# Down projection, first three column blocks: the low part of the weights made by ScalarE and an accumulating DMA

## The chip, the cores and the metric

The kernel runs on one core of one Trainium2 chip. The metric is the device time of one execution in microseconds; of several executions the median is taken. The engines are PE (TensorE), DVE (VectorE), ACT (ScalarE), POOL (GpSimd) and SP (SyncE, which here issues every DMA of the kernel before). Each engine runs its own instructions in order and waits for the others by semaphores. The DMA engines, 16 for the core, move data on their own once an issue has reached them.

## The reference

One layer of a streaming encoder on 256 tokens of width 2048, all in float32. Cut to what matters here:

```python
def conv_glu(h, w_up, conv_w, conv_b, w_down):
    ug = h @ w_up                                  # [256, 2 * 5632]
    gate, up = ug[..., :D_FF], ug[..., D_FF:]
    gate = causal_depthwise_conv(gate, conv_w) + conv_b
    return (silu(gate) * up) @ w_down              # [256, 5632] @ [5632, 2048]

def reference(...):
    ...                                            # two token mixers, w_in, projections, w_out
    h = h + conv_glu(rmsnorm(h, norm_ffn), w_up, conv_w, conv_b, w_down)
    return rmsnorm(h, norm_final)
```

The change concerns the last product, with `w_down`.

## The kernel before, in words

Every large product is made of float32 operands that are split in two: hi is the value rounded to the matmul's reduced float32 format (fp32r), lo is the exact rest, value minus hi. `mm3` (lines 87 to 90) then issues three matmuls per pair of tiles: hi times hi, hi times lo, lo times hi. Activations are split once; weights are split as they come.

The weights come in blocks of 1 MiB, [128, 2048] float32, four tiles of 128 rows of the weight matrix (K tiles) by 512 columns each. `load_split` (lines 92 to 103) has SP load one block into a tile `raw` (three buffers), and then for each half of it, [128, 1024], has ACT write hi as a copy of raw (line 80), and DVE write lo as raw minus hi (line 81). The pools of hi and lo have three buffers each, so three halves are in hand at a time, and a half's buffers are used again by the half three later.

`product` (lines 211 to 225) walks over the K tiles of one block of 512 output columns. Each half holds two K tiles; for each, and for each of the two blocks of 128 tokens, `mm3` adds into that token block's PSUM tile: twelve matmuls of 512 columns a half. There the activations' tile (`u` in the trace) is the stationary operand and hi or lo of the weights is the moving one, so of the three matmuls only that of line 89 reads lo.

The down projection is four such column blocks over 44 K tiles, that is 11 weight blocks each. The first three go through `product` (lines 615 to 618), each followed by `residual`, which adds h and squares it. The fourth (lines 627 to 658) is written out by hand, with `load_split` for ten of its blocks and a split of its own for the last. The order of each engine's instructions is set by a scheduler when the program is built, not by the order of the lines alone: the splits for the first halves of the down projection are placed among the last instructions of the up projection, and their matmuls follow its last without a pause.

Of the kernel before, what the change touches and what calls it, by code (L numbers as in the profile page):

```python
# [13 lines left out]
ALU = mybir.AluOpType  # L14
# [16 lines left out]
UNIT = 2048  # L31
WARM = 10  # products of zeros

# columns of the packed per-partition vectors
C_NFFN = 0
# [8 lines left out]
def tile_block(ctx: ExitStack, tc: tile.TileContext, ins, out):  # L44
# [32 lines left out]

# [1 line left out]
    def split(hi, lo, src):  # L79
# [11 lines left out]

    def load_split(src):
        """One 1 MiB block of weights as two halves of (hi, lo), each [P, 1024]."""
        raw = wraw.tile([P, 2048], F32, tag="raw", name=nm("raw"))
        sp.dma_start(raw, src)
        got = []
        for h in range(2):
            r = raw[:, h * 1024 : (h + 1) * 1024]
            hi = wsplit.tile([P, 1024], F32R, tag="hi", name=nm("hi"))
            lo = wsplit.tile([P, 1024], F32R, tag="lo", name=nm("lo"))  # L100
            split(hi, lo, r)
            got.append((hi, lo))
        return got

# [1 line left out]
    def rsqrt(v, n):  # L106
# [11 lines left out]

# [1 line left out]
    side = deque()  # L120
# [8 lines left out]

# [1 line left out]
    warm = const.tile([P, NB], BF16, tag="warm", name="warm")  # L131
# [6 lines left out]

# [1 line left out]
    nmix = const.tile([P, KT], F32, tag="nmix", name="nmix")  # L140
# [31 lines left out]

# [1 line left out]
    trig = const.tile([P, 2 * TB * 64], F32, tag="trig", name="trig")  # L174
# [34 lines left out]

# [1 line left out]
    def product(src, start, nk, lhs_h, lhs_l, ready=None, bank=None):  # L211
        """src[start + i] are blocks of four K tiles; returns one PSUM tile per token block."""
        ps = [(bank or acc_tile)() for _ in range(TB)]
        for g in range(nk // 4):
            halves = [ready[g, 0], ready[g, 1]] if ready else load_split(src[start + g])
            for hf, (wh, wl) in enumerate(halves):
                for j in range(2):
                    kt = g * 4 + hf * 2 + j
                    s = slice(j * NB, (j + 1) * NB)
                    for tb in range(TB):  # L220
                        ah = lhs_h(kt)[:, tb * P : (tb + 1) * P]
                        al = lhs_l(kt)[:, tb * P : (tb + 1) * P]
                        mm3(ps[tb], ah, al, wh[:, s], wl[:, s], kt == 0, kt == nk - 1)
            tick()
        return ps
# [3 lines left out]

# [1 line left out]
    def rotary_block(nb, qk, base, late=False, ready=None, bank=None):  # L231
# [38 lines left out]

# [1 line left out]
    ret_h = [unit(F32R) for _ in range(2)]  # L272
    ret_l = [unit(F32R) for _ in range(2)]

    def retention(half, qk, vh, vl):
        dec = unit()
        sp.dma_start(dec[:, : 4 * 384], ins["decay"][:, half * 4 * 384 : (half + 1) * 4 * 384])
        o_all = unit()
        mv = small.tile([P, 8, 2], F32, tag="mv", name=nm("mv"))
        scores = {}  # L280

        def score(hd):
            q3 = [x[:, hd * T : (hd + 1) * T] for x in qk]
            k3 = [x[:, (4 + hd) * T : (5 + hd) * T] for x in qk]
            ps = aux_tile()
            mm3(ps[:, :T], k3[0][:, :P], k3[1][:, :P], q3[0], q3[1], True, True)
            mm3(ps[:, T : T + P], k3[0][:, P:], k3[1][:, P:], q3[0][:, P:], q3[1][:, P:], True, True)
            s = t2k(384, F32)
            sh = t2k(384, F32R)
            sl = t2k(384, F32R)  # L290
            dve.tensor_tensor(s, ps[:, :384], dec[:, hd * 384 : (hd + 1) * 384], ALU.mult)
            split(sh, sl, s)
            scores[hd] = (sh, sl)

        def output(hd):
            sh, sl = scores.pop(hd)
            po = aux_tile()
            v0 = slice(hd * DV, (hd + 1) * DV)
            v1 = slice(1024 + hd * DV, 1024 + (hd + 1) * DV)
            mm3(po[:, :DV], sh[:, :P], sl[:, :P], vh[:, v0], vl[:, v0], True, True)  # L300
            mm3(po[:, DV:], sh[:, P : 2 * P], sl[:, P : 2 * P], vh[:, v0], vl[:, v0], True, False)
            mm3(po[:, DV:], sh[:, 2 * P :], sl[:, 2 * P :], vh[:, v1], vl[:, v1], False, True)
            for tb in range(TB):
                st = small.tile([P, 6], F32, tag="st", name=nm("st"))
                dve.bn_stats(st, po[:, tb * DV : (tb + 1) * DV])
                dve.bn_aggr(mv[:, hd * 2 + tb, :], st)
            # o_all is [token block][head][channel], as the gate is
            ov = o_all.rearrange("p (b h e) -> p b h e", b=TB, h=4)
            act.activation(ov[:, :, hd, :], po.rearrange("p (b e) -> p b e", b=TB), AF.Copy)

        for hd in range(4):
            side.append(lambda hd=hd: score(hd))
            if hd:
                side.append(lambda hd=hd: output(hd - 1))
        side.append(lambda: output(3))
        return o_all, mv

# [35 lines left out]

    # x and its sums of squares follow the first weights, so the first two blocks leave PSUM late
    for _ in range(KT // 4 + 2):
# [22 lines left out]

# [1 line left out]
    ph, pl = unit(F32R), unit(F32R)  # L380
# [63 lines left out]

# [1 line left out]
    sgp = [unit(), unit()]  # L446
# [6 lines left out]

# [1 line left out]
    mg_h = [unit(F32R) for _ in range(2)]  # L455
# [29 lines left out]

# [1 line left out]
    ht_h = [unit(F32R) for _ in range(2)]  # L487
# [32 lines left out]
    def norm2():  # L520
        ss = small.tile([P, TB], F32, tag="ss", name="ss")
        dve.tensor_reduce(ss, ssq2, mybir.AxisListType.X, ALU.add)
        r2 = rms(ss)
        # 1/rms of each token along the free axis, on all partitions
        pb = aux_tile()
        for tb in range(TB):
            dg = tmp.tile([P, P], F32, tag="dg", name=nm("dg"), bufs=1)
            dve.tensor_scalar(dg, ident, r2[:, tb : tb + 1], None, ALU.mult)
            pe.matmul(pb[:, tb * P : (tb + 1) * P], ones, dg, start=True, stop=True)
        dve.tensor_copy(rb, pb[:, :T])  # L530

    side.append(norm2)

# [1 line left out]
    ah = [unit(F32R) for _ in range((NFF + 7) // 8)]  # L535
    al = [unit(F32R) for _ in range((NFF + 7) // 8)]
    for j in range(NFF):
        # the first pair alternates by halves of K, since the last K tiles of h are still on their way
        ps = [acc_tile() for _ in range(2)] if j == 0 else [acc_tile()] * 2
# [32 lines left out]

# [1 line left out]
    gf = unit()  # L574
# [4 lines left out]
    def residual(tb, nb, ps):  # L579
        """h's block of columns, its squares, and the block times the last gain."""  # L580
        n = NB // 2 if nb == 3 else NB
# [12 lines left out]
    def finish(tb, last):  # L594
# [3 lines left out]
        dve.tensor_scalar(v, ssq3[:, tb, 4:5], 1.0 / D, a, ALU.mult, ALU.add)  # L598
        # the root's reciprocal, and a step of Newton's method on it
        r = small.tile([P, 1], F32, tag="fin_r", name=nm("r"))  # L600
# [14 lines left out]
    for nb in range(3):  # L615
        ps = product(ins["w_down"], nb * 11, NFF, lambda k: kview(ah, k), lambda k: kview(al, k))
        for tb in range(TB):
            residual(tb, nb, ps[tb])
# [5 lines left out]

    # the last block of columns: its last eight K tiles go to one token block, then to the other
    LAST = 8
# [33 lines left out]

# [1 line left out]
def _blocks(w, np):  # L662
    """[K, N] -> [N / 512 * K / 512][partition][four K tiles x 512 columns]."""
    k, n = w.shape
# [8 lines left out]
def _arrays(np, x, norm_mix, w_in, w_pool_group, pool_scale, w_pool_proj, ret_gn_gain,  # L673
# [27 lines left out]
    a["norm_final"] = np.asarray(norm_final).reshape(1, D)  # L701
    # constants
    t = np.arange(T)
# [38 lines left out]
```

## Time and profile before

| | |
|---|---|
| time of the runs, median of 2 (lowest to highest) | 1502.15 us (1502.11 to 1502.2) |
| the profiled execution, span from first to last instruction | 1499.8 us |
| between that span and the median of the runs | 2.35 us |
| DMA in the whole run | 287.17 MB, mean 191 GB/s |
| first matmul of the down projection | at 1251.9 us |
| mean granted TensorE clock | 0.999 |

The profile gives for each engine its busy time, and for groups of instructions their count, mean duration and the idle time before them with what ended it. In rows of the timeline the first number is the start and the second the length, both in microseconds; `<-` in brackets names the instruction whose end released the row. Matmuls overlap, so their spacing, not their length, is what one costs. For the profiled execution the page gives the span; the time around it (start-up before the first instruction and completion after the last) is taken as the 2.35 us of the table.

### The profile page before, as it was taken

How to read it: one execution, taken by the hardware profiler on the slowest of the kernel's cores; microseconds unless marked ns; L12 is line 12 of the kernel's file. 1: busy time of each engine (PE TensorE's matmuls, PEld its weight loads, DVE VectorE, ACT ScalarE, POOL GpSimd, SP SyncE). 2: the span in 40 equal slices, each digit the busy share in tenths (PEclk: the TensorE clock that was granted, in tenths of full speed). 3: DMA queues.
4: the chain of work that ended last, by engine and by line, in shares of the span. 5: the costliest groups of instructions: out<-in, count | busy, mean ns of one | idle time of the engine just before them, and what ended most of it. 6: DMA issues, size and time to landing. Idle time of an engine off the chain costs nothing.

```text
span 1499.8 us, 20866 instructions
## 1 busy us (share of the span) xinstructions
PE 1488.2 (99%) x8694; PEld 1319.2 (88%) x8694; DVE 886.6 (59%) x1142; ACT 676.5 (45%) x811; POOL 0.2 (0%) x4
## 2 busy tenths in 40 slices
PE   9999999999999999999999999999999999999997
PEld 6888888888888888888899999999999998888886
DVE  6765865675444455555666666666666665455454
ACT  6545444464444434435544444444444444344343
POOL 0000000000000000000000000000000000000000
PEclk9999999999999999999999999999999999999999
DMA  9554455464455555655444555445554455555553
GB/s 346 200 213 162 177 202 184 168 226 163 178 189 193 195 196 193 231 194 190 175 181 185 181 186 182 184 182 183 184 182 186 180 186 210 194 196 196 197 193 115
DMA packets 42718, 287.17 MB, mean 191 GB/s; under 512 B 4992, under 2 KB 5632, under 8 KB 9088
## 3 DMA queue, kind: packets, MB, share of 16 engines
q1 hardware_dynamic: 42624, 285.84, 52.1%
q8 instruction: 68, 1.11, 0.3%
q14 instruction: 26, 0.21, 0.0%
HBM read 283.73 MB, written 2.10 MB: 191 GB/s over the span
## 4 chain that ended last, share of the span: by engine, by line
PE 98%; DVE 1%; DMA 0%; ACT 0%; SPq 0%; issue 0%; ACTq 0%
PE acc L88 32%; PE acc L90 31%; PE acc L89 31%; PE aux L89 1%; PE aux L90 1%; PE aux L88 1%; DMA raw<-in_w_in 0%; PE aux L246 0%; PE aux L476 0%; PE aux L339 0%; PE aux L505 0%; DVE lo L81 0%; PE aux L404 0%; ACT hi L80 0%; DVE u L85 0%; PE aux L408 0%
## 5 line engine op out<-in xcount | busy, mean ns | idle before, releaser
L81 DVE TENSOR_TENSOR lo<-raw,hi 128x1024 fp32r<-128x1024 f32 (+1 forms) x526 | 635.2, 1209 | 516.3 <-ACT hi L80 515.6
L80 ACT ACTIVATE hi<-raw 128x1024 fp32r<-128x1024 f32 (+1 forms) x526 | 549.4, 1046 | 694.2 <-PE acc L90 446.6
L88 PE MATMUL acc<-hi,u 128*128 128x512 f32 x1336 | 523.6, 392 | 0.0
L90 PE MATMUL acc<-hi,u 128*128 128x512 f32 x1336 | 520.5, 390 | 0.0
L89 PE MATMUL acc<-lo,u 128*128 128x512 f32 x1336 | 520.2, 389 | 0.0
L88 PE MATMUL acc<-u,hi 128*128 128x256 f32 x1408 | 398.7, 283 | 0.0
L90 PE MATMUL acc<-u,lo 128*128 128x256 f32 x1408 | 398.5, 283 | 0.0
L89 PE MATMUL acc<-u,hi 128*128 128x256 f32 x1408 | 398.4, 283 | 0.0
L90 PEld LDWEIGHTS acc<-hi,u 128*128 128x128 f32 x1336 | 250.8, 188 | 52.9
L89 PEld LDWEIGHTS acc<-lo,u 128*128 128x128 f32 x1336 | 251.0, 188 | 50.9
L88 PEld LDWEIGHTS acc<-hi,u 128*128 128x128 f32 x1336 | 250.9, 188 | 50.2
L89 PEld LDWEIGHTS acc<-u,hi 128*128 128x128 f32 x1408 | 270.3, 192 | 0.0
L88 PEld LDWEIGHTS acc<-u,hi 128*128 128x128 f32 x1408 | 270.3, 192 | 0.0
L90 PEld LDWEIGHTS acc<-u,lo 128*128 128x128 f32 x1408 | 270.3, 192 | 0.0
L556 DVE TENSOR_TENSOR t<-acc,rb 128x512 f32<-128x512 f32 x43 | 29.7, 692 | 26.6 <-PE acc L90 26.6
L80 ACT ACTIVATE u<-t 128x256 fp32r<-128x256 f32 x44 | 18.4, 417 | 52.7 <-DVE t L569 52.7
L81 DVE TENSOR_TENSOR u<-t,u 128x256 fp32r<-128x256 f32 x44 | 18.5, 425 | 19.8 <-ACT u L80 19.4
L84 ACT ACTIVATE u<-aux,vecs 128x256 fp32r<-128x256 f32 x40 | 18.6, 468 | 23.1 <-DVE u L85 22.1
L85 DVE SCALAR_TENSOR_TENSOR u<-aux,vecs,u 128x256 fp32r<-128x256 f32 x40 | 19.1, 480 | 8.7 <-ACT u L84 8.7
L567 DVE SCALAR_TENSOR_TENSOR t<-t,vecs,t 128x254 f32<-128x254 f32 x44 | 21.3, 483 | 1.6
L568 ACT ACTIVATE t<-t,vecs 128x256 f32<-128x256 f32 x44 | 21.9, 497 | 0.0
L566 DVE SCALAR_TENSOR_TENSOR t<-t,vecs,t 128x255 f32<-128x255 f32 x44 | 21.1, 478 | 0.0
(129 smaller groups left out, 457.8 us busy)
## 6 DMA issues: line engine op xcount, KB each, us to landing
raw<-in_w_up SPq DMA_DIRECT2D x88, 1024.0 KB, 4.8
raw<-in_w_in SPq DMA_DIRECT2D x84, 1024.0 KB, 4.8
raw<-in_w_down SPq DMA_DIRECT2D x44, 1024.0 KB, 4.8
raw<-in_w_ret_proj SPq DMA_DIRECT2D x16, 1024.0 KB, 4.8
raw<-in_w_out SPq DMA_DIRECT2D x16, 1024.0 KB, 4.8
raw<-in_w_pool_proj SPq DMA_DIRECT2D x8, 1024.0 KB, 4.8
u<-in_x SPq DMA_DIRECT2D x4, 1024.0 KB, 8.1
raw<-in_w_in SPq DMA_DIRECT2D x7, 512.0 KB, 7.8
```

Source lines behind the costliest of these rows:

```text
L80: act.activation(hi, src, AF.Copy)
L81: dve.tensor_tensor(lo, src, plain(hi), ALU.subtract)
L84: act.activation(hi, src, AF.Copy, scale=scale)
L85: dve.scalar_tensor_tensor(lo, src, scale, plain(hi), ALU.mult, ALU.subtract)
L88: pe.matmul(o, ah, bh, start=start, stop=False)
L89: pe.matmul(o, ah, bl, start=False, stop=False)
L90: pe.matmul(o, al, bh, start=False, stop=stop)
L556: dve.tensor_tensor(gu.rearrange("p (s t) -> p s t", s=2), ps[0].rearrange("p (s t) -> p s t", s=2), rb.unsqueeze(1).broadcast_to([P, 2, T ...
L566: dve.scalar_tensor_tensor(c[:, 1:], g[:, : T - 1], w[1], c[:, 1:], ALU.mult, ALU.add)
L567: dve.scalar_tensor_tensor(c[:, 2:], g[:, : T - 2], w[0], c[:, 2:], ALU.mult, ALU.add)
L568: act.activation(c, c, AF.Silu, bias=vec(C_CONVB + j))
```

## The change

`load_split` gets a switch `by_dma`, which `product` hands on, and which the first three column blocks of the down projection set. With it, DVE's subtraction goes: ACT writes hi as before, and ACT also writes lo as a copy of raw with scale -1, rounded to fp32r like hi, which makes it minus hi. A DMA that POOL issues then adds the raw half, 512 KB in SBUF, onto lo in place, which makes it raw minus hi. All other places, the fourth column block among them, keep the subtraction.

```diff
-    def load_split(src):
+    def load_split(src, by_dma=False):
         raw = wraw.tile([P, 2048], F32, tag="raw", name=nm("raw"))
         sp.dma_start(raw, src)
...
             hi = wsplit.tile([P, 1024], F32R, tag="hi", name=nm("hi"))
             lo = wsplit.tile([P, 1024], F32R, tag="lo", name=nm("lo"))
-            split(hi, lo, r)
+            if by_dma:
+                act.activation(hi, r, AF.Copy)
+                act.activation(lo, r, AF.Copy, scale=-1.0)
+                nc.gpsimd.dma_start(lo, r, accum_op=ALU.add)
+            else:
+                split(hi, lo, r)
...
-    def product(src, start, nk, lhs_h, lhs_l, ready=None, bank=None):
+    def product(src, start, nk, lhs_h, lhs_l, ready=None, bank=None, by_dma=False):
...
-            halves = [ready[g, 0], ready[g, 1]] if ready else load_split(src[start + g])
+            halves = [ready[g, 0], ready[g, 1]] if ready else load_split(src[start + g], by_dma)
...
-        ps = product(ins["w_down"], nb * 11, NFF, lambda k: kview(ah, k), lambda k: kview(al, k))
+        ps = product(ins["w_down"], nb * 11, NFF, lambda k: kview(ah, k), lambda k: kview(al, k), by_dma=True)
```

The rest of the diff takes comments out and moves line numbers by seven or so. How the instructions now stand on three engines, early in the down projection's first column block; in the brackets are the engines whose semaphores an instruction waits for (DMAHW with a number is the landing of one of SP's DMAs, DMASW of one of POOL's). ACT before, five halves one after another:

```order
L80 ACTIVATE hi_11296<-raw_11294 128x1024 [waits DMAHW7_49,PE_49,Activation_49]
L80 ACTIVATE hi_11300<-raw_11294 128x1024 [waits DVE_49,PE_49]
L80 ACTIVATE hi_11330<-raw_11328 128x1024 [waits DMAHW0_49,DVE_49,PE_49]
L80 ACTIVATE hi_11334<-raw_11328 128x1024 [waits DVE_49,PE_49]
L80 ACTIVATE hi_11364<-raw_11362 128x1024 [waits DMAHW1_49,DVE_49,PE_49]
```

ACT now, at the same blocks, three halves:

```order
L105 ACTIVATE lo_11303<-raw_11300 128x1024 [waits DMAHW7_49,DMASW3_49,PE_49]
L104 ACTIVATE hi_11302<-raw_11300 128x1024 [waits PE_49,Activation_49]
L105 ACTIVATE lo_11308<-raw_11300 128x1024 [waits DMASW4_49,PE_49]
L104 ACTIVATE hi_11307<-raw_11300 128x1024 [waits PE_49,Activation_49]
L105 ACTIVATE lo_11339<-raw_11336 128x1024 [waits DMAHW0_49,DMASW5_49,PE_49]
L104 ACTIVATE hi_11338<-raw_11336 128x1024 [waits PE_49,Activation_49]
```

ACT has two copies a half where it had one, and the scheduler puts that of lo ahead of that of hi; the wait on DMASW is for the accumulate that last wrote the same buffer. POOL, which had no DMA before, has 66 rows of this kind one behind another:

```order
L106 DMA lo_11303<-raw_11300 128x1024 [waits DMAHW7_49,DMASW3_49,Activation_49]
L106 DMA lo_11308<-raw_11300 128x1024 [waits DMASW4_49,Activation_49]
L106 DMA lo_11339<-raw_11336 128x1024 [waits DMAHW0_49,DMASW5_49,Activation_49]
L106 DMA lo_11344<-raw_11336 128x1024 [waits DMASW6_49,Activation_49]
L106 DMA lo_11375<-raw_11372 128x1024 [waits DMAHW1_49,DMASW7_49,Activation_49]
```

Each waits for ACT's copy of lo. The loads on SP, before and then now:

```order
L95 DMA raw_11294<-in_w_down 128x2048 [waits DMAHW3_49,DVE_49]
L95 DMA raw_11328<-in_w_down 128x2048 [waits DMAHW4_49,DVE_49]
L95 DMA raw_11362<-in_w_down 128x2048 [waits DMAHW5_49,DVE_49]
L95 DMA raw_11396<-in_w_down 128x2048 [waits DMAHW7_49,DVE_49]
L95 DMA raw_11430<-in_w_down 128x2048 [waits DMAHW0_49,DVE_49]
```

```order
L97 DMA raw_11300<-in_w_down 128x2048 [waits DMASW1_49,DMAHW3_49,DMASW0_49,Activation_49]
L97 DMA raw_11336<-in_w_down 128x2048 [waits DMASW3_49,DMAHW4_49,DMASW2_49,Activation_49]
L97 DMA raw_11372<-in_w_down 128x2048 [waits DMASW5_49,DMAHW5_49,DMASW4_49,Activation_49]
L97 DMA raw_11408<-in_w_down 128x2048 [waits DMASW7_49,DMAHW7_49,DMASW6_49,Activation_49]
L97 DMA raw_11444<-in_w_down 128x2048 [waits DMASW1_49,DMAHW0_49,DMASW0_49,Activation_49]
```

The loads stand in the same order; each now waits for the landing of the two accumulates that read the raw buffer it takes, where it waited for DVE. PE's matmuls stand in the same order but for a handful, and those of line 89 that are first to read a lo wait for its DMA.

## The prediction

> **What bounds the kernel now.** I read the page's first part, then its chain of waits (fourth part), to learn which engine sets the end.
>
> ```profile
> span 1499.8 us, 20866 instructions
> PE 1488.2 (99%) x8694; PEld 1319.2 (88%) x8694; DVE 886.6 (59%) x1142; ACT 676.5 (45%) x811; POOL 0.2 (0%) x4
> PE 98%; DVE 1%; DMA 0%; ACT 0%; SPq 0%; issue 0%; ACTq 0%
> ```
>
> TensorE (PE) is busy for 99% of the span and is 98% of the chain. So nothing that the other engines do costs time now, and the change can't win time by taking work off VectorE (DVE): only a stretch in which PE waits can change the end. Of GpSimd (POOL) the page shows four instructions and no DMA, so the operation that is added has no row of its own in this trace.
>
> Next the stage that is edited. The groups of instructions and the waits in the stretch from 1262 to 1440 us, which lies inside the first three column blocks of the down projection:
>
> ```profile
> L89 PE MATMUL acc<-lo,u 128*128 128x512 f32 x263 | 102.3, 389 | 0.0
> L81 DVE TENSOR_TENSOR lo<-raw,hi 128x1024 fp32r<-128x1024 f32 x66 | 80.9, 1226 | 90.9 <-ACT hi L80 90.8
> L80 ACT ACTIVATE hi<-raw 128x1024 fp32r<-128x1024 f32 x66 | 70.0, 1061 | 104.3 <-PE acc L90 104.2
> ...
> ACT hi L80 <- PE acc L90: 104.2, 65, 1.7
> DVE lo L81 <- ACT hi L80: 90.8, 65, 1.5
> ...
> SPq L95 <- DVE lo L81: 166.1, 33, 5.1
> ```
>
> PE has no idle time here. ScalarE (ACT) waits 104.2 us for PE to give hi and lo buffers back; DVE waits for ACT; SP's queue waits for DVE to be done with the raw block. Everything follows PE, and the question is by how much it runs ahead. For that I follow one half block through the timeline. The first matmul of the stage stands at 1251.92, and twelve make a half, so the fifth half ends with the matmul at 1265.33 and the eighth begins at 1270.99; with three buffers the eighth half takes the fifth's.
>
> ```profile
> 1251.92 0.40 PE L88 MATMUL acc<-hi,u 128*128 128x512 f32 x1
> ...
> 1265.10 0.39 PE L89 MATMUL acc<-lo,u 128*128 128x512 f32 x1
> 1265.33 0.39 PE L90 MATMUL acc<-hi,u 128*128 128x512 f32 x1
> ...
> 1265.75 1.06 ACT L80 ACTIVATE hi<-raw 128x1024 fp32r<-128x1024 f32 x1 [1.61 <-PE acc L90]
> ...
> 1266.85 1.23 DVE L81 TENSOR_TENSOR lo<-raw,hi 128x1024 fp32r<-128x1024 f32 x1 [1.45 <-ACT hi L80]
> ...
> 1268.47 1.06 ACT L80 ACTIVATE hi<-raw 128x1024 fp32r<-128x1024 f32 x1 [1.66 <-PE acc L90]
> ...
> 1270.99 0.39 PE L88 MATMUL acc<-hi,u 128*128 128x512 f32 x1
> ...
> 1271.22 0.39 PE L89 MATMUL acc<-lo,u 128*128 128x512 f32 x1
> ```
>
> One half takes 1268.47 - 1265.75 = 2.72 us, a matmul 0.227 us, a block of two halves 5.44 us. The lo of the eighth half is ready at 1266.85 + 1.23 = 1268.08 and first read at 1271.22: today it has **3.1 us to spare**.
>
> **The change part by part.** Removed: 66 subtractions on DVE (3 column blocks x 11 weight blocks x 2 halves) at 1226 ns, 80.9 us. They lie beside PE's matmuls, so their going is worth nothing. Added on ACT: 66 copies with scale -1. The nearest row is the hi copy of the same shape, 1061 ns, so 70.0 us, and ACT's work per half goes to 2.12 us of the 2.72: it still fits. Since lo no longer needs hi, the copy of lo can start as soon as the last matmul that reads the old lo is over (1265.10 + 0.39 = 1265.49, about 0.03 us later by the gap seen at hi), and it ends at 1265.52 + 1.06 = 1266.58. The hi copy behind it ends near 1267.6, with 3.4 us to spare before 1270.99: no cost.
>
> Then comes what decides: a DMA from POOL reads raw (512 KB) and lo (512 KB) and writes lo (512 KB), and PE waits for its landing. From 1266.58 to 1271.22 there are **4.64 us** of cover. If the accumulate takes D from ACT's end to its landing, every run of three halves becomes longer by D - 4.64, because a buffer's next turn can't start before PE has read its last one. 66 halves are 22 such turns, so
>
> lost time = 22 x (D - 4.64), where D is above 4.64, else none.
>
> The stage's first three halves are prepared during the up projection, and the stall there is of the same size as in any turn; I don't add one. The last column block goes back to DVE, with its 3.1 us.
>
> D is not in this trace. The rows around it:
>
> ```profile
> raw<-in_w_down SPq DMA_DIRECT2D x33, 1024.0 KB, 4.8
> ...
> u<-in_x SPq DMA_DIRECT2D x2, 1024.0 KB, 8.3
> raw<-in_w_in SPq DMA_DIRECT2D x2, 256.0 KB, 3.6
> ```
>
> These are DMA issues with KB each and median us to landing, the first from the down projection, the others from the first 60 us, when many loads were queued together. Lower end: bytes written alone, 512 KB, lie between the 256 KB row (3.6) and the 1024 KB row (4.8), so about 4, which is under the cover: nothing lost. Upper end: three passes (raw, lo, and lo written) one after another at the 1024 KB row's 4.8 each, 14.4 us: 22 x 9.76 = 215 us. Between them I count reads: 1 MiB, as in the 1024 KB rows, which gives 4.8 us with free engines and 8.3 us beside other loads. How free are they? The stage's line in the view by stretches, whose last three columns are granted clock, DMA share and GB/s, and the bandwidth line of the first 60 us in 1.5 us slices:
>
> ```profile
> 1262.00:1440.00 178.00, 178.00 (x787) 147.40 (x786) 87.87 (x81) 74.24 (x80) 0.00 (x0) 1.00 0.53 193
> ...
> GB/s 0 120 171 309 274 314 318 422 408 406 404 400 403 434 418 415 344 350 426 426 333 415 431 431 268 426 245 85 306 317 0 208 404 87 76 229 387 38 78 339
> ```
>
> The raw loads alone keep the 16 engines busy for 53%, that is 0.53 x 5.44 = 2.9 us for the 1 MiB of a block. Two accumulates add 2 MiB of reads per block. At the same price that is 5.7 us more, 8.6 in all for a block of 5.44; at the highest rate seen, 434 GB/s, 1 MiB takes 2.4 us and the block 7.2. So the DMA engines would be overbooked by 1.8 to 3.2 us per block, 33 blocks: +59 to +104 us. The engines are not free, so I take the **8.3 us** row: 22 x (8.3 - 4.64) = 80.5 us, which falls in the middle of what the bytes give. The two limits describe the same transfers and are not added.
>
> A rule of the Trainium skill speaks for no loss. Its page "DMA: Bandwidth & Descriptors", section "Anatomy of one DMA", gives a GpSimd-issued DMA about 2.0 us plus bytes over 436 GB/s, and "Collectives: The Full Stack", at "Why ReduceScatter is half of AllGather", says that an inline add costs two source reads. An estimate from both is 2.0 + 2.4 = 4.4 us, under the cover, and the sum would be 1502. The trace agrees for the lone load (4.8 beside the rule's 4.4) and not for loads that share the engines (8.3).
>
> What is queued behind the new waits. Behind the accumulate on POOL stand only later accumulates: 66 with one per 2.72 us or slower, against 0.33 us that SP's queue takes for an issue (the one-issue row below); POOL's own time per issue has no row, and is part of D. Behind the copy of lo on ACT stands hi of the same half, and at the end of a column block the two squares of the residual, for which PE does not wait. SP's raw load now waits for the two accumulates of the block three earlier, in place of DVE:
>
> ```profile
> 1249.24 0.33 SPq L575 DMA_DIRECT2D u<-in_norm_final  x1
> ...
> 1262.72 32.91 SPq L95 DMA_DIRECT2D raw<-in_w_down  x7
> ```
>
> Seven issues in 32.91 us are one per 5.44. A raw slot comes free when the second accumulate of its block lands, about when PE starts that half, and its next content is wanted by ACT when PE ends the half two later: three halves, 8.2 us today and 11.8 us when stretched by 3.66, against a landing of 4.8 to 8.3. That is covered, and costs if the cover goes only what the landing is above it.
>
> **The rivals.**
> (1) *The accumulate hides: not slower.* If D stays at or below 4.64 us, the lo chain is still ready when PE asks, and PE keeps 0.227 us per matmul: 1502 us. It speaks for it that the lone 1024 KB load lands in 4.8 and that POOL has nothing else to do; against it that the engines are half booked. Up to D = 6.0, 22 x 1.36 = 30 us are lost, which is 2%.
> (2) *The inline add is slower than its reads.* With D at the three passes' 14.4 us the time is 1502 + 215 = 1717, and more if the pieces of a transfer are not overlapped. Nothing in the trace shows an add in a DMA, so nothing excludes it.
> (3) *PE's clock falls in the pauses.* The lost time may come as one pause of 3.7 us per three halves. The start of the run shows matmuls after idle time:
>
> ```profile
> 1.18 3.81 PE L137 MATMUL aux<-warm 128*128 128x512 bf16 x10 [1.18 <-DVE warm L132]
> ```
>
> Ten in 3.81 us are 0.38 us each against 0.227 in the stage. If ten after each pause run so, 22 x 10 x 0.154 = 34 us come on top: 1617. The page "TensorE: Matmul & The Clock Gate", section "HAM oscillation", states this rule, with the full clock lost after about 3.4 us idle; the slower first ten agree with it.
> (4) *Faster.* It would need PE to run quicker without DVE's reads; PE's idle is 0.0 and its spacing steady, so I see no room. That the add isn't done as described I exclude: the order of instructions has 66 such DMAs.
>
> **How the numbers follow.** Span 1499.8 + 80.5 = 1580.3; the median of the runs, 1502.15, lies 2.35 us above the span, so 1582.7, say **1583**. Chances: forecast, a loss of 30 to 150 us, 0.52; hidden (1) 0.17; slow add (2) 0.21; clock (3) 0.08; faster 0.02. A measurement of this kernel can tell about 2% (30 us) from no change. Slower by over 2%: 0.52 + 0.21 + 0.08 = 0.81; within 0.17; faster 0.02. The range starts at 1512 (D = 5.1), leaving out the best half of (1) and the faster case, about 0.1, and ends at 1740, just above the three passes, leaving out about 0.1 of (2).
>
> **What would show it.** PE's share falls to about 94%, with idle time before L89 (the first reader of lo) put down to the POOL DMA; ACT waits for PE at lo; DVE nearly idle from 1252 us; DMA share near 0.9 or above in the stage; the accumulate's landing near 8 us; the up projection and the last column block unchanged. I am wrong if PE shows no idle time at L89 (rival 1), if the landing is over 12 us or if PE waits for raw by way of ACT (rival 2), or if matmuls behind a pause take 0.38 us (rival 3).

## The result, and the profile after

| | before | after |
|---|---|---|
| median of the runs | 1502.15 us | 1611.72 us (1607.6 to 1615.84) |
| ratio, 95% interval | | 1.073 (1.0713 to 1.0747) |
| span of the profiled execution (after: that of the run of 1607.6 us) | 1499.8 us | 1605.7 us |
| PE busy in it | 1488.2 us | 1524.6 us |
| PE not busy in it | 11.6 us | 81.1 us |

The change makes the kernel slower by 7.3%. The page after, from its first, second, fourth and sixth part (slices of 40.1 us; the down projection starts in the 32nd):

```profile
span 1605.7 us, 21072 instructions
PE 1524.6 (95%) x8694; PEld 1335.2 (83%) x8694; DVE 806.8 (50%) x1076; ACT 738.8 (46%) x877; POOL 57.1 (4%) x70
...
PE   9999999999999999999999999999999777777797
...
PEclk9999999999999999999999999999999898998899
DMA  9554554454555556555555555555555999999963
...
PE 81%; DMA 11%; issue 6%; DVE 1%; POOL 0%; ACT 0%; SPq 0%; POOLq 0%; ACTq 0%
...
raw<-in_w_down SPq DMA_DIRECT2D x44, 1024.0 KB, 7.2
lo<-raw POOLq DMA_DIRECT2D x66, 512.0 KB, 7.9
```

Everything is in the edited stage: there PE falls to 7 tenths, the granted clock to 8 tenths in four of its slices, and the DMA engines go from 5 tenths to 9. Before it nothing moved. The 105.9 us that the span grew by are 69.5 us in which PE does nothing (81.1 - 11.6) and 36.4 us by which its matmuls take longer (1524.6 - 1488.2).

The groups and waits of the stage, 1262 to 1530 us:

```profile
L89 PE MATMUL acc<-lo,u 128*128 128x512 f32 x255 | 113.2, 444 | 61.1 <-DMA lo<-raw 60.9
L105 ACT ACTIVATE lo<-raw 128x1024 fp32r<-128x1024 f32 x63 | 66.7, 1058 | 142.3 <-PE acc L89 142.3
L106 POOL DMA_DIRECT2D lo<-raw x63 | 54.2, 860 | 218.2 <-ACT lo L105 189.9 <-DMA lo<-raw 13.3 <-ACT u L80 9.5
...
POOL lo L106 <- ACT lo L105: 189.9, 56, 8.1
...
ACT lo L105 <- PE acc L89: 142.3, 61, 8.6
...
PE acc L89 <- DMA lo<-raw: 60.9, 27, 4.4
```

That is the chain of the prediction, closed: ACT waits for PE to give lo back, POOL for ACT, PE at line 89 for the landing. What such a pause does to PE is seen in the timeline:

```profile
1411.29 0.86 POOL L106 DMA_DIRECT2D lo<-raw  x1 [1.86 <-ACT lo L105]
...
1413.88 0.50 PE L89 MATMUL acc<-lo,u 128*128 128x512 f32 x1 [3.52 <-DMA lo<-raw]
...
1416.04 0.63 PE L89 MATMUL acc<-lo,u 128*128 128x512 f32 x1
...
1416.47 0.63 PE L90 MATMUL acc<-hi,u 128*128 128x512 f32 x1
```

Soon after a pause of 3.52 us the matmuls stand 0.43 us apart (1416.04 to 1416.47), not 0.227, for some 3 us.

The yardstick for the experiments is the stretch from 1270 to 1430 us in the view by stretches: the number of matmuls (first x) over 24 gives the weight blocks done, then clock and DMA share, and GB/s last. Before and after:

```profile
1270.00:1430.00 160.00, 160.00 (x708) 132.48 (x707) 76.69 (x67) 65.04 (x67) 0.00 (x0) 1.00 0.54 196
```

```profile
1270.00:1430.00 160.00, 121.99 (x457) 92.43 (x455) 2.69 (x4) 78.91 (x82) 33.27 (x39) 0.91 1.02 250
```

708 matmuls are 29.5 blocks, 5.42 us each; 457 are 19.0 blocks, **8.40 us each**, with the DMA engines busy all the time (a share of 1.00, or a little above it in these rows).

### The profile page after: what moved, and what is told of

The parts are those of the page before. It is cut to its first block, busy times and chain, and to the rows that moved or that the text cites. A ratio compares the mean times of both kernels' runs of the same rounds, so it can differ in the third digit from the quotient of the medians.

```text
span 1605.7 us, 21072 instructions
## 1 busy us (share of the span) xinstructions
PE 1524.6 (95%) x8694; PEld 1335.2 (83%) x8694; DVE 806.8 (50%) x1076; ACT 738.8 (46%) x877; POOL 57.1 (4%) x70
## 4 chain that ended last, share of the span: by engine, by line
PE 81%; DMA 11%; issue 6%; DVE 1%; POOL 0%; ACT 0%; SPq 0%; POOLq 0%; ACTq 0%
PE acc L89 26%; PE acc L90 26%; PE acc L88 26%; DMA lo<-raw 10%; PE aux L89 1%; PE aux L90 1%; PE aux L88 1%; DMA raw<-in_w_in 0%; POOL lo L106 0%; DMA raw<-in_w_down 0%; PE aux L346 0%; PE aux L483 0%; PE aux L253 0%; ACT lo L105 0%; DVE lo L81 0%
## 5 line engine op out<-in xcount | busy, mean ns | idle before, releaser
L81 DVE TENSOR_TENSOR lo<-raw,hi 128x1024 fp32r<-128x1024 f32 (+1 forms) x460 | 554.3, 1206 | 512.7 <-ACT hi L80 512.0
L80 ACT ACTIVATE hi<-raw 128x1024 fp32r<-128x1024 f32 (+1 forms) x460 | 479.4, 1044 | 592.0 <-PE acc L90 346.6
L89 PE MATMUL acc<-lo,u 128*128 128x512 f32 x1336 | 535.0, 400 | 69.2 <-DMA lo<-raw 68.9
L88 PE MATMUL acc<-hi,u 128*128 128x512 f32 x1336 | 533.1, 399 | 0.0
L90 PE MATMUL acc<-hi,u 128*128 128x512 f32 x1336 | 531.2, 398 | 0.0
L89 PEld LDWEIGHTS acc<-lo,u 128*128 128x128 f32 x1336 | 256.8, 192 | 135.4 <-DMA lo<-raw 83.3
L90 PEld LDWEIGHTS acc<-hi,u 128*128 128x128 f32 x1336 | 257.2, 193 | 54.1
L88 PEld LDWEIGHTS acc<-hi,u 128*128 128x128 f32 x1336 | 257.4, 193 | 53.4
L105 ACT ACTIVATE lo<-raw 128x1024 fp32r<-128x1024 f32 x66 | 69.8, 1058 | 142.3 <-PE acc L89 142.3
L106 POOL DMA_DIRECT2D lo<-raw x66 | 56.9, 862 | 1470.7 <-ACT lo L105 1442.4
L592 DVE TENSOR_TENSOR u<-acc,u 128x512 f32<-128x512 f32 (+1 forms) x10 | 5.6, 583 | 180.2 <-PE acc L90 180.2
L104 ACT ACTIVATE hi<-raw 128x1024 fp32r<-128x1024 f32 x66 | 68.7, 1042 | 2.9 <-PE acc L90 1.2
```

The lines of the kernel that those rows point to most:

```text
L80: act.activation(hi, src, AF.Copy)
L81: dve.tensor_tensor(lo, src, plain(hi), ALU.subtract)
L88: pe.matmul(o, ah, bh, start=start, stop=False)
L89: pe.matmul(o, ah, bl, start=False, stop=False)
L90: pe.matmul(o, al, bh, start=False, stop=stop)
L104: act.activation(hi, r, AF.Copy)
```

## The experiments

Two theories fit that. **Theory A**: the chain of waits, with a landing of 7.9 us against 4.64 us of cover, and the clock that falls in the pauses. **Theory B**: the 16 DMA engines are full, and their 8.4 us per block set the pace whatever the cover. The prediction had worked out both limits and taken the chain's number, which lies within the range of the other. The diffs below are shortened: dots and comments stand for what they leave out.

**deep: more cover, all accumulates.**

```diff
+        odd[0] ^= by_dma
+        lo2 = unit(F32R) if by_dma and odd[0] else None   # spare [128, 2048] tiles, every second block
...
-            lo = wsplit.tile([P, 1024], F32R, tag="lo", name=nm("lo"))
+            lo = lo2[:, h * 1024 : (h + 1) * 1024] if lo2 is not None else wsplit.tile(...)
```

> The changed kernel, but every second weight block takes its lo from spare tiles, so that a lo buffer comes free at least four halves ahead instead of three: the cover for copy, accumulate and landing grows from 4.64 us to about 10 us. Theory A (a chain of waits: PE gives lo back, copy, accumulate landing in 7.9 us, PE; and a slowed clock after the pauses): landing is now under the cover, so pauses at line 89 nearly vanish, clock back to 1.00, 1502 to 1520 us. Theory B (the 16 DMA engines are full: 8.6 us of transfers per weight block against 5.44 us of matmuls, whatever the buffers): no change, 1600 to 1615 us, DMA share 1.0 in the stage.

Measured: 1585.17 us, ratio 1.0552 (1.0535 to 1.0569). 27 of the 110 us went, not all of them. The yardstick's line, the issues from 1270 to 1500 us, and the waits from 1260 to 1500 us:

```profile
1270.00:1430.00 160.00, 127.60 (x495) 98.47 (x494) 2.68 (x4) 80.76 (x86) 34.69 (x41) 0.93 1.02 265
```

```profile
raw<-in_w_down SPq DMA_DIRECT2D x29, 1024.0 KB, 8.9
lo<-raw POOLq DMA_DIRECT2D x30, 512.0 KB, 10.7
u<-raw POOLq DMA_DIRECT2D x28, 512.0 KB, 9.6
```

```profile
ACT u L112 <- DMA raw<-in_w_down: 70.2, 13, 6.6
PE acc L88 <- ACT hi L111: 35.4, 13, 3.4
...
SPq L99 <- DMA u<-raw: 105.3, 16, 16.5
```

495 matmuls are 7.76 us a block, at share 1.02. With more in flight every transfer lands later (accumulates near 10 us, loads 8.9 where they took 7.5 in the same stretch after), and PE now waits for hi, which ACT can't make because the raw block is late. Theory A's 1502 to 1520 is wrong for this kernel; theory B's "no change" is nearer, though 15 us too high. Two things qualify it. The share is 1.02 in both kernels, but 265 GB/s move here and 250 after, so a full share is not one fixed price a block. And the loads now wait for the accumulates to leave one of the three raw buffers (the row of SPq), so a chain through those buffers is a rival to the full engines here: no run has more of them.

**filler: matmuls on zeros where PE paused.**

```diff
+                        if by_dma and j == 0 and tb == 0:
+                            for _ in range(5):
+                                pe.matmul(fill, warm[:, :P], warm, start=True, stop=True)
                         mm3(ps[tb], ah, al, wh[:, s], wl[:, s], kt == 0, kt == nk - 1)
```

> The changed kernel with five more matmuls on zeros ahead of each half in the three column blocks (330 more, about 1.1 us a half), into a bank that nobody reads. Theory A: the fillers stand where the pauses were and keep the clock up, so a turn of three halves is bounded by the matmuls (11.5 us) or the chain (11.8 us): about 1580 us, clock 1.00, less than the changed kernel's 1612 with more work. Theory B: a block needs 8.6 us of the DMA engines and the matmuls with fillers only 7.6: stays at 1600 to 1615 us.

Measured: 1611.0 us, ratio 1.0723 (1.0707 to 1.0739): 330 more matmuls and the same time as the changed kernel.

```profile
1270.00:1430.00 160.00, 145.82 (x633) 98.04 (x632) 2.68 (x4) 75.44 (x78) 31.80 (x37) 1.00 0.99 242
```

The clock is back at 1.00, and 185 of these 633 matmuls are fillers, so 448 real ones, 8.57 us a block. The fillers took the place of pauses and slow matmuls almost one for one: their 46.4 us (the row below, from the same stretch) are what PE's pauses and its real matmuls lost.

```profile
L233 PE MATMUL aux<-warm 128*128 128x512 bf16 x185 | 46.4, 381 | 0.0
```

So the fallen clock was not what set the time there: with it mended, the block still takes as long, the engines still full (0.99). A filler costs 0.25 us (46.4 / 185) and not the 0.22 that the expectation reckoned with; theory A's number becomes 1502 + 22 x 15 x 0.25 = 1585 us, still 26 below the measured one. That goes by the median landing, so the run alone does not part the theories cleanly.

**noload: the accumulates without the loads.**

```diff
-            raw = wraw.tile([P, 2048], F32, tag="raw", name=nm("raw"))
-            sp.dma_start(raw, src)
+            # by_dma: the first block's raw tile for all 33
+            raw = held_raw[0]
```

> The changed kernel, but the three column blocks use one weight block that is loaded once, instead of 33 (32 loads of 1 MiB are left out). If the landing of 7.9 us comes from sharing the engines with the loads: accumulates land near the 4.6 us minimum, D about 4.9, loss 22 x 0.3 = 6 us, about 1510 us under theory A; under theory B two accumulates take 5.6 us of the engines per block of 5.44, also about 1506 us. If the accumulate is slow by itself: landing stays near 7.9 us and the time at 1580 us or above.

Measured: 1528.31 us, ratio 1.0174 (1.0158 to 1.0189). The DMA issues of the stretch from 1270 to 1430 us, and its line:

```profile
lo<-raw POOLq DMA_DIRECT2D x54, 512.0 KB, 4.6
```

```profile
1270.00:1430.00 160.00, 153.71 (x643) 117.23 (x642) 5.37 (x8) 109.83 (x116) 46.42 (x54) 1.00 0.93 176
```

Without the loads an accumulate lands in 4.6 us; the other 3.3 of the 7.9 are the sharing with them. The expected 1510 us was too low: at D = 4.6 + 0.28 (from ACT's end to POOL's row) the formula leaves a pause of 0.24 us per turn. The stretch has 65 matmuls fewer than before, 0.8 us for each of its 18 turns, and the first wait of the stage is 5.68 us.

**halfload: half of the loads.**

```diff
-        sp.dma_start(raw, src)
+        sp.dma_start(raw[:, :1024], src[:, :1024])   # by_dma: both halves are made from it
```

> The changed kernel, but of each weight block only the first 512 KB are loaded, and both halves are made from them (the second half of the weights is left out). Theory B: 1.4 + 5.6 = 7.0 us of the engines per block, 33 x 1.6 = 52 us over before, about 1555 us. Theory A alone has no number for it but a landing between 4.6 us (no loads) and 7.9 us (full loads): 6.2 us, D 6.5, 22 x 1.9 = 41 us, about 1545 us; the two do not part here, and the run gives the middle of the dose between the changed kernel and the one without loads.

Measured: 1578.21 us, ratio 1.0499 (1.0482 to 1.0517), landing 6.9 us, above both numbers. It lies between no loads (1528) and full loads (1612), nearer the full ones.

```profile
1270.00:1430.00 160.00, 128.23 (x512) 98.67 (x511) 5.36 (x8) 88.11 (x94) 36.21 (x42) 0.96 0.98 213
```

512 matmuls are 7.50 us a block, at a share of 0.98: with half of the loads the engines are still nearly full. Over the three doses of loads (none, half, all) a block takes 5.97, 7.50 and 8.40 us at shares of 0.93, 0.98 and 1.02.

**copy: the same DMA without the addition.**

```diff
-                nc.gpsimd.dma_start(lo, r, accum_op=ALU.add)
+                nc.gpsimd.dma_start(lo, r)
```

> The changed kernel with a plain copy of raw onto lo in place of the accumulate (the sum is left out, so lo is wrong; 512 KB read per DMA instead of 1 MiB). Theory B by bytes read: 2.9 + 2 x 1.4 = 5.7 us of the engines per block against 5.44 of matmuls, about 1510 us, landing near 5.5 us. If the price of the accumulate is that of a GpSimd DMA as such and not of its second read: engines stay full, landing near 7.9 us, 1600 us.

Measured: 1555.59 us, ratio 1.0355 (1.033 to 1.0379). Its issues and DMA share from 1260 to 1500 us:

```profile
q0 software_dynamic: 8930, 32.51, 37.6%
...
raw<-in_w_down SPq DMA_DIRECT2D x36, 1024.0 KB, 5.7
lo<-raw POOLq DMA_DIRECT2D x62, 512.0 KB, 4.4
```

A copy of 512 KB takes 0.376 x 240 / 62 = 1.46 us of the 16 engines; the accumulate in the changed kernel, by the same stretch, 0.659 x 240 / 57 = 2.77 us (57 of them, 65.9%). That is 1.9 copies, the price of two reads; the run does not part the second read from the addition, which the copy lacks as well. In the yardstick's stretch:

```profile
1270.00:1430.00 160.00, 138.96 (x568) 109.93 (x567) 5.35 (x8) 95.68 (x102) 24.27 (x46) 0.96 0.89 306
```

Half the price brought half of the loss, not the 8 us that theory B's sum left: the engines' share is 0.89 and a block takes 6.76 us. PE still pauses for landings (31.1 us in 18 waits from 1260 to 1500 us), which are 4.4 us in the median and reach 8.6.

**half: half of the accumulates.**

```diff
-            if by_dma:
+            if by_dma and h == 0:
```

> Only the first half of each weight block takes its lo by the accumulate, the second half keeps the subtraction: 33 accumulates. Theory B: 2.9 + 2.8 = 5.7 us of the engines per block, about 1510 us. Theory A: buffers pass from a half with an accumulate to one with a subtraction, whose 3.1 us of spare time take up what a landing up to 7.7 us loses: 1502 to 1505 us.

Measured: 1572.45 us (1564.49 to 1584.79), ratio 1.0475 (1.0419 to 1.0531). Both theories' numbers are wrong. The engines have room, and still:

```profile
1270.00:1430.00 160.00, 132.52 (x541) 104.19 (x539) 33.20 (x31) 71.86 (x76) 18.91 (x22) 0.96 0.83 222
```

A share of 0.83 and 7.1 us a block: that is no full engine, so theory B does not explain it. Theory A's mechanism does, but my use of it was wrong: the spare time of a half made by subtraction can't be lent, since PE runs in order and the accumulate's cover is only what lies between PE's giving back and PE's next use. The median landing, 6.1 us, is above the 4.64 us of cover. My estimate of what that costs: two accumulates fall in each turn and share its surplus, (6.1 + 0.28 - 4.64) / 2 = 0.87 us a block, which makes 6.3 us. Of the 0.8 us that the measured 7.1 lies above that, landings over the median (up to 9.5 us) and the clock (0.96) may be the causes; no run parts them.

**halfdeep: both edits.** This is the cross of `deep` and `half`.

> Both edits of the earlier runs together: only the first half of each block takes the accumulate (2.9 + 2.8 = 5.7 us of the engines per block of 5.44, DMA share 0.79 in the earlier run), and every second block takes lo from spare tiles, so that each accumulate has about 10 us of cover. Theory A: the landing of 6.1 us is covered, pauses vanish, clock back to 1.00: 1502 to 1510 us, against 1572 without the cover. Theory B alone, with the loss set by the engines: 1510 us at most from the sum of transfers, or no change from 1572 if something else of the transfers sets it.

Measured: 1525.38 us (1524.25 to 1536.69), ratio 1.0179 (1.0139 to 1.0218).

```profile
1270.00:1430.00 160.00, 152.15 (x661) 123.09 (x660) 38.10 (x35) 83.10 (x90) 23.27 (x27) 1.00 0.95 269
```

5.81 us a block. Where the engines have room, cover takes away most of the loss (1572 to 1525); where they are full, a quarter of it (1612 to 1585). About half of what is left, some 11 of the span's 22.7 us, lies at one place:

```profile
1261.46 0.79 PE L89 MATMUL acc<-u,u 128*128 128x512 f32 x1 [8.52 <-DMA u<-raw]
```

That is PE's first wait for an accumulate, 8.5 us long, at the change of stages. The changed kernel has it too:

```profile
1259.14 0.80 PE L89 MATMUL acc<-lo,u 128*128 128x512 f32 x1 [6.35 <-DMA lo<-raw]
```

The rest are waits of 0.2 to 1.5 us for other accumulates, spread over the stage.

**noloaddeep: cover, and no loads.** `deep` and `noload` together.

> All 66 accumulates, the loads left out (one weight block is used for all, as in the earlier run), and the cover of about 10 us. Two accumulates at 2.8 us are 5.6 us of the engines per block of 5.44. Theory A: the landing of 4.6 us is covered: 1502 to 1510 us, against 1528 without the cover. Theory B: 33 x 0.16 = 5 us, about 1507 us. If the 26 us of the earlier run are neither, the time stays near 1528.

Measured: 1515.15 us, ratio 1.0085 (1.007 to 1.0101).

```profile
1270.00:1430.00 160.00, 160.00 (x707) 132.55 (x706) 5.35 (x8) 119.06 (x126) 50.92 (x59) 1.00 1.01 191
```

In the stretch nothing is lost: 707 matmuls against 708 before, with all accumulates and a share of 1.01. Two accumulates take as long as the matmuls of a block, 5.4 us, and with enough cover that fits. The 13 us are the first wait, 10.6 us here, and the slow matmuls behind it:

```profile
1262.82 0.80 PE L89 MATMUL acc<-u,u 128*128 128x512 f32 x1 [10.60 <-DMA u<-raw]
```

**late: the accumulates begin at the fifth weight block** (otherwise `halfdeep`).

```diff
-            halves = ... load_split(src[start + g], by_dma)
+            halves = ... load_split(src[start + g], by_dma and (start, g) >= (0, 4))
```

> As the run with half the accumulates and the longer cover (1525 us), but the first four of the 33 weight blocks keep the subtraction, so that the 29 accumulates begin after the loads at the change of stages (two weight blocks and the final gain within a few us) are over. If the pause of 8.5 us at the first accumulate, with the slowed matmuls behind it, is an entry price of that place: 1504 to 1512 us. If every first accumulate of POOL lands late, wherever it stands: the landing of 10 us is covered here by the longer cover or nearly, 1502 to 1515; then the first landing in the trace is again near 10 us and not near 6.

Measured: 1516.41 us (1508.16 to 1520.61), ratio 1.0084 (1.006 to 1.0107): 9 us less than `halfdeep`, and above both expected ranges. The long pause is gone; the longest left, by the timeline, is

```profile
1293.62 0.50 PE L89 MATMUL acc<-lo,u 128*128 128x512 f32 x1 [2.20 <-DMA lo<-raw]
```

The first accumulate lands in 7.2 us here and the second in 9.5, so a first one is not late as such. In the profiled executions the place accounts for the 9 us: `halfdeep` loses some 11 us at the entry and 11 in the short waits behind it, `late` nothing at the entry and 14.5 in such waits (up to the 2.20 us above) and one spell of slow matmuls. So half of the accumulates, with the longer cover, still cost short waits.

**lolast: the readers of lo last in each half.**

```diff
-                        mm3(ps[tb], ah, al, wh[:, s], wl[:, s], kt == 0, kt == nk - 1)
+                        pe.matmul(ps[tb], ah, wh[:, s], start=kt == 0, stop=False)
+                        pe.matmul(ps[tb], al, wh[:, s], start=False, stop=False)
...                      # then, once per half, the four matmuls that read wl
```

> The changed kernel with the matmuls that read lo placed last in each half (eight of hi first, then four of lo): the cover grows by six matmuls, 1.36 us. Theory A: 22 x 1.36 = 30 us less, about 1580 us. Theory B: the engines stay full, 1600 to 1612 us.

Measured: 1596.94 us, ratio 1.0634 (1.0618 to 1.0649), 15 us under the changed kernel: half of theory A's gain. As with `deep`, more cover helps, but by less than it adds.

**junk: accumulates beside the subtraction.**

```diff
-                nc.gpsimd.dma_start(lo, r, accum_op=ALU.add)
+            split(hi, lo, r)
+            nc.gpsimd.dma_start(junk[:, h * 1024 : (h + 1) * 1024], r, accum_op=ALU.add)
```

> Subtraction on DVE as in the kernel before, and the same 66 accumulating DMAs beside it, into a spare tile that nobody reads, each waiting only for its raw block and for the accumulate two earlier. Theory A: PE waits for no accumulate, at most for raw blocks held a little longer: 1502 to 1520 us. Theory B: the engines have 8.6 us of transfers per block, raw loads come late, PE waits for them: about 1600 us.

Measured: 1660.82 us, ratio 1.1045 (1.1027 to 1.1064), slower than the change itself, at a DMA share of 0.91 from 1260 to 1500 us. The waits of that stretch say why it answers neither theory:

```profile
POOL u L107 <- DMA u<-raw: 197.2, 47, 7.6
ACT hi L80 <- DMA raw<-in_w_down: 182.5, 22, 9.0
```

Each accumulate writes the same spare half as the one two before and waits for its landing (10.2 us in the median), and holds its raw block meanwhile, so the loads came late. The experiment had built a new chain, through the spare tile and the raw buffers: two accumulates at a time, one block per landing (365 matmuls in the yardstick's stretch, 10.5 us a block).

## Why the prediction was right, and where a term was off

- **PE bounds the kernel, work taken off DVE wins nothing.** Held: DVE lost 80 us of work (886.6 to 806.8), and no stretch became faster.
- **ACT's second copy fits.** Held: 1058 ns (1061 forecast), and ACT waits 142.3 us for PE.
- **D.** Taken as 8.3 us from a load beside other loads; the landing is 7.9 us from POOL's row, 0.28 us after ACT's end, so 8.2. That it was the row under sharing and not the lone one is shown by `noload`: 4.6 us. Counting the accumulate at its reads was right to a few per cent: 2.77 us of the engines against the 2.9 of a 1 MiB load.
- **Lost time 22 x (D - 4.64).** The chain and D were right, the loss was too small: 80.5 us forecast, 105.9 measured in the span. The mis-sized term is the length of a block. The forecast took it from the chain alone, 5.44 + 80.5 / 33 = 7.88 us; 8.40 are measured, which over 33 blocks is a loss of 98 us, and most of the rest, some 8 us, lies at the entry. In PE's own account 69.5 us of the growth are idle and 36.4 us are longer matmuls, for which the sum had nothing.
- **Clock.** Given 0.08 as a rival of its own, priced at 34 us on top, with a sign: matmuls behind a pause at 0.38 us. The sign came, at 0.43 us, beside the forecast's pauses. So 0.08 was too low: the pauses and the clock belong in one case. That 1617 lies near the measured 1612 is partly luck. The price counted 220 slow matmuls at 0.154 us extra; the timeline from 1252 to 1545 us shows about 125 at 0.2, in some 15 spells. Nor is it a term to be added to the others: with the clock kept up, `filler` took as long. The Trainium skill ("TensorE: Matmul & The Clock Gate", section "HAM oscillation") warns of idle gaps over about 3.4 us. The trace agrees for the pause of 3.52 us, but 3.4 us is no limit in it: matmuls slowed after a pause of 2.11 us, and not after one of 2.97:

```profile
1313.24 0.50 PE L89 MATMUL acc<-lo,u 128*128 128x512 f32 x1 [2.97 <-DMA lo<-raw]
...
1315.42 0.39 PE L89 MATMUL acc<-lo,u 128*128 128x512 f32 x1
1315.64 0.39 PE L90 MATMUL acc<-hi,u 128*128 128x512 f32 x1
...
1324.31 0.50 PE L89 MATMUL acc<-lo,u 128*128 128x512 f32 x1 [2.11 <-DMA lo<-raw]
...
1327.04 0.63 PE L89 MATMUL acc<-lo,u 128*128 128x512 f32 x1
1327.47 0.63 PE L90 MATMUL acc<-hi,u 128*128 128x512 f32 x1
```

- **Engines overbooked, 7.2 to 8.6 us a block.** 8.40 measured, and the prices measured here give 2.9 + 2 x 2.77 = 8.4. I had said that this limit and the chain describe the same transfers, and had taken the chain's lower number; with all 66 accumulates most of the loss stays when the chain is relieved. `deep` shows it (7.76 us at share 1.02 with the cover doubled), and `filler` fits it. But 0.64 us a block went with the cover, so the 8.4 are no fixed floor; and that the 7.76 are the engines, and not the chain through the raw buffers, is likely by the share but not shown. Where the engines have room the chain is what costs, shown by the pair `half` and `halfdeep`.
- **Raw loads behind the accumulates, "covered".** Held: from 1262 to 1530 us one wait of 2.0 us for a raw block (POOL's) is all. With the longer cover of `deep` they become what ACT waits for.
- **The entry.** "The stall there is of the same size as in any turn; I don't add one" failed: the first wait is 6.35 us in the changed kernel, against 3.66 forecast for a turn and 2.9 measured (60.9 us over some 21 turns), and eleven slow matmuls follow it, some 2 us more.
- **Rival 1** (the accumulate hides) would have needed both: 10 us of cover and no loads (`noloaddeep`, 1515, all of the loss at the entry). **Rival 2** (the addition slower than its reads) fell: 4.6 us without the loads, and 2.77 us of the engines where two copies take 2.92.
- The Trainium skill's fit with two reads ("DMA: Bandwidth & Descriptors", section "Anatomy of one DMA"), estimated at 4.4 us, agrees with the landing of 4.6 without the loads and not with the 7.9 beside them. The prediction could compare it only with loads, which SP issues and not GpSimd.

Left open: how far the fallen clock costs time of its own where the engines have room (`half` has 21.2 us of longer matmuls and 45.0 of idle in its span's 66.2, and no run holds the clock up there), and what more raw buffers would bring in `deep`. No version beats the kernel before; with PE busy for 99% of it, none of these could.

## What to carry to other kernels

An accumulate in SBUF cost the DMA engines as much as two reads here (2.77 us against 1.46 for a copy): before moving work there, add up the engines' time per stage with that price, as one adds up an engine's instructions, and compare that sum with the chain. The larger of the two is a floor rather than the time: `copy` and `half` came out above both (6.76 us a block against 5.8, and 7.1 against 6.3), since single landings lie far from their median. A lone landing is no price where loads share the engines. And where an asynchronous step stands between giving a buffer back and using it again, it is the number of buffers that buys its cover, which helped much while the engines had room (47 of 70 us) and little when they were full (27 of 110).

## What the runs showed that I had not expected

- The same 512 KB accumulate lands in 4.6 us without the loads, 7.9 us beside them and near 10 us with more of them in flight.
- A share of 0.83 of the DMA engines did not mean that 17% were to be had: with three buffers a block took 7.1 us instead of 5.4, waiting for landings.
- POOL's row for an issue takes 0.86 us for the accumulate and 0.53 for the plain copy, where SP's takes 0.33.
